# A first transfer of 4 rows ahead of the 16-row transfers in a DMA-fed relu-and-sum kernel

## The chip, the cores and the metric

The kernel runs on one core of one Trainium2 chip. In what follows, ACT is the scalar engine, DVE the vector engine, and SP the engine that here only issues transfers. A chunk is the rows that one transfer brings to a buffer. A transfer lands when its semaphore, a counter that engines wait for, tells that all its data are there.

The metric is device time in microseconds (us). Every run quoted here was fast (granted clock 1.0 in all), so only like runs are compared. The profile covers a span about 1.5 us shorter than the device time (161.4 us against 162.92 in the run profiled before). Times within a profile count from the start of that span.

## The reference

```python
x = np.random.randn(32, 512, 1024).astype(np.float32)   # 67.1 MB
relu_x = np.maximum(x, 0)
out = np.sum(relu_x, axis=-1).astype(np.float32)         # one number per row of 1024
```

There are 16384 rows, so 128 rows on each of the 128 partitions. A row is 4 KB. Each byte is read once and used once.

## The kernel before

The rows of a partition lie one behind the other in memory, so "16 rows per partition" is one run of 64 KB per partition. Seven transfers of 16 rows go round three buffers. A tail of 8, 4, 2 and 1 rows and two half rows follows in one of those buffers (the last half row in a small array of its own), so that little compute is left after the last byte.

```python
BIG = 16; NBIG = 7; NTWO = 6; NB = 3
STEPS = [4, 5, 7]; MIXED = [3, 4, 5]; TAIL = [8, 4, 2, 1]; LAST = [512, 512]

tb = NBIG % NB
for c in range(NBIG + 1):                       # issued from SP
    if c >= NB:
        sp.wait_ge(s_dve, 3 * (c - NB + 1))     # the chunk three earlier is consumed
    if c < NBIG:
        sp.dma_start(out=buf[:, c % NB, :, :],
                     in_=xv[:, c * BIG : (c + 1) * BIG, :]).then_inc(s_in[c], 16)
# ... tail transfers into buf[:, tb], each with a semaphore of its own ...

for c in range(NTWO):                           # chunks 0 to 5
    b, steps = c % NB, STEPS if c < NTWO - 1 else MIXED
    act.wait_ge(s_in[c], 16)
    # ... chunk 5: 2 rows go to DVE alone and 2 to ACT alone ...
    r = 0
    for i, n in enumerate(steps):
        t = buf[:, b, r : r + n, :]
        act.activation(t, t, AF.Relu).then_inc(s_act, 1)          # relu in place
        dve.wait_ge(s_act, 3 * c + i + 1)
        dve.tensor_reduce(out=res[:, c * BIG + r : c * BIG + r + n], in_=t,
                          axis=X, op=ALU.add).then_inc(s_dve, 1)  # sums of n rows
        r += n

for c in range(NTWO, NBIG):                     # chunk 6: row by row, both engines
    act.wait_ge(s_in[c], 16)
    dve.wait_ge(s_in[c], 16)
    for i in range(BIG):
        (on_act if i % 2 else on_dve)(*row(c, i))   # relu and sum in one instruction
# ... tail pieces the same way; the last half row is summed by DVE; then res goes out ...
```

## Time and profile before

The median was 162.84 us of 3 runs before the prediction, and 162.94 us of 4 with the run beside the result.

| What | Value | Read from |
|---|---|---|
| DMA engines busy | 97.0% of the span | page, queue part |
| DVE / ACT busy | 76% / 63% | page, busy part |
| 64 KB packet on one DMA engine | 2418 ns | the trace's packet records |
| First packet starts / last input packet ends | 1.73 / 158.5 us | the same |
| Last input to the end of the span | about 3 us | chain of waits, timeline |

From the page of the kernel before: busy time by engine, the busy tenths of the DMA engines and their rate in 40 equal slices of 4.03 us, and the queue's share of 16 engines' span.

```profile
DVE 122.0 (76%) x56; ACT 101.0 (63%) x55; POOL 0.2 (0%) x4
...
DMA  7969979979979979979979979979979979899992
GB/s 260 504 292 504 471 341 487 487 325 487 487 325 487 471 309 520 471 309 520 487 309 504 487 325 487 487 325 487 487 325 487 487 325 487 374 422 414 406 406 74
...
q1 hardware_dynamic: 2016, 67.18, 97.0%
```

A packet is booked in the slice in which it starts. A 64 KB packet lasts more than half a slice, so the rate swings between 300 and 500. The swings are no holes: the busy share is 97%.

SP waits by the waits view (engine and line, whom it waited for, us in total, times, longest). SP issues the transfers:

```profile
SPq L58 <- DVE res L101: 99.9, 4, 42.8
SPq L132 <- DVE last L82: 34.7, 1, 34.7
SPq L64 <- DVE res L101: 19.0, 1, 19.0
```

This looks like a transfer queue held up by DVE, and it is not. The list of DMA issues gives, for the seven 16-row transfers, the median time from issue to landing:

```profile
buf<-in_x_dram SPq DMA_DIRECT2D x7, 36.4
```

The movement of one such transfer takes about 19.4 us (8 packets of 2418 ns on each engine). It lands 36.4 us after its issue because about 17 us of earlier transfers are queued ahead of it.

The end of the chain of waits (start us, us, what), and four lines of DVE's timeline near the end (start us, us, the instruction, and in brackets the idle time before it and what ended that). The first line of the second fence is the first row of chunk 6, then come the first row of the 8-row piece, the first of the 4-row piece, and the last half row.

```profile
124.16 34.13 DMA buf<-in_x_dram
158.29 0.02 issue
158.31 0.73 ACT buf L79 x2
159.04 0.02 issue
159.07 0.69 DVE last L82 x2
```

```profile
139.27 1.22 DVE L82 TENSOR_SCALAR_CACHE_REDUCE buf<-buf 128x1024 f32<-128x1024 f32 x1 [1.74 <-DMA buf<-in_x_dram]
...
148.99 1.22 DVE L82 TENSOR_SCALAR_CACHE_REDUCE buf<-buf 128x1024 f32<-128x1024 f32 x1 [0.51 <-DMA buf<-in_x_dram]
...
153.88 1.22 DVE L82 TENSOR_SCALAR_CACHE_REDUCE buf<-buf 128x1024 f32<-128x1024 f32 x1 [0.25 <-DMA buf<-in_x_dram]
...
159.07 0.69 DVE L82 TENSOR_SCALAR_CACHE_REDUCE last<-last 128x513 f32<-128x513 f32 x1 [0.19 <-ACT buf L79]
```

DVE waits for data before every piece: it keeps up. The compute that nothing hides is the last half rows' (0.73 and 0.69 us). The start of the kernel, by contrast, shows the two engines idle for a long time: ACT's first activation starts at 23.13 us, DVE's first reduction at 26.78.

```profile
23.13 14.04 ACT L99 ACTIVATE buf<-buf 128x4096 f32<-128x4096 f32 x3 [21.13 <-DMA buf<-in_x_dram]
26.78 9.85 DVE L101 TENSOR_REDUCE res<-buf 128x4 f32<-128x4096 f32 x2 [26.78 <-ACT buf L99]
```

### The profile page before, as it was taken

How to read it: one execution, taken by the hardware profiler on the slowest of the kernel's cores; microseconds unless marked ns; L12 is line 12 of the kernel's file. 1: busy time of each engine (PE TensorE's matmuls, PEld its weight loads, DVE VectorE, ACT ScalarE, POOL GpSimd, SP SyncE). 2: the span in 40 equal slices, each digit the busy share in tenths (PEclk: the TensorE clock that was granted, in tenths of full speed). 3: DMA queues.
4: the chain of work that ended last, by engine and by line, in shares of the span. 5: the costliest groups of instructions: out<-in, count | busy, mean ns of one | idle time of the engine just before them, and what ended most of it. 6: DMA issues, size and time to landing. Idle time of an engine off the chain costs nothing.

```text
span 161.4 us, 143 instructions
## 1 busy us (share of the span) xinstructions
DVE 122.0 (76%) x56; ACT 101.0 (63%) x55; POOL 0.2 (0%) x4
## 2 busy tenths in 40 slices
DVE  0000003998969898798979989699899999598995
ACT  3000029992499906998089960999429980496972
POOL 0000000000000000000000000000000000000000
DMA  7969979979979979979979979979979979899992
GB/s 260 504 292 504 471 341 487 487 325 487 487 325 487 471 309 520 471 309 520 487 309 504 487 325 487 487 325 487 487 325 487 487 325 487 374 422 414 406 406 74
DMA packets 2016, 67.18 MB, mean 416 GB/s; under 512 B 224, under 2 KB 352, under 8 KB 736
## 3 DMA queue, kind: packets, MB, share of 16 engines
q1 hardware_dynamic: 2016, 67.18, 97.0%
HBM read 67.11 MB, written 0.07 MB: 416 GB/s over the span
## 4 chain that ended last, share of the span: by engine, by line
DMA 69%; ACT 18%; DVE 10%; SPq 1%; issue 0%
DMA buf<-in_x_dram 69%; ACT buf L99 17%; DVE res L101 9%; SPq L64 1%; ACT buf L79 0%; DVE last L82 0%; SPq L58 0%
## 5 line engine op out<-in xcount | busy, mean ns | idle before, releaser
L101 DVE TENSOR_REDUCE res<-buf 128x4 f32<-128x4096 f32 (+3 forms) x18 | 100.4, 5603 | 34.9 <-ACT buf L99 34.9
L99 ACT ACTIVATE buf<-buf 128x4096 f32<-128x4096 f32 (+3 forms) x18 | 80.8, 4553 | 47.7 <-DMA buf<-in_x_dram 47.7
L79 ACT ACTIVATE buf<-buf 128x1024 f32<-128x1024 f32 (+1 forms) x18 | 18.4, 1021 | 9.7 <-DMA buf<-in_x_dram 9.7
L82 DVE TENSOR_SCALAR_CACHE_REDUCE buf<-buf 128x1024 f32<-128x1024 f32 x18 | 21.0, 1217 | 2.7 <-DMA buf<-in_x_dram 2.5
L79 ACT ACTIVATION_READ_ACCUMULATOR buf<-buf 128x1 f32 x18 | 3.4, 187 | 0.0
L99 ACT ACT_TABLE_LOAD x1 | 1.3, 1283 | 0.7 <-PEq L147 0.7
L82 DVE DVE_READ_ACCUMULATOR buf<-buf 128x1 f32 x18 | 1.5, 84 | 0.0
L82 DVE TENSOR_SCALAR_CACHE_REDUCE last<-last 128x513 f32<-128x513 f32 x1 | 0.7, 690 | 0.2 <-ACT buf L79 0.2
L147 POOL MEMSET const-bfloat16-1.0<- 128x1 bf16 x1 | 0.1, 102 | 0.0
L147 POOL MEMSET const-uint8-127<- 128x1 uint8 x1 | 0.1, 101 | 0.0
L147 POOL MEMSET const-float32-0.0<- 128x1 f32 x1 | 0.1, 99 | 0.2 <-issue 0.2
L147 POOL MEMSET const-float32-1.0<- 128x1 f32 x1 | 0.1, 98 | 0.0
L82 DVE DVE_READ_ACCUMULATOR last<-last 128x1 f32 x1 | 0.1, 83 | 0.0
## 6 DMA issues: line engine op xcount, KB each, us to landing
buf<-in_x_dram SPq DMA_DIRECT2D x1, 4096.0 KB, 26.7
buf<-in_x_dram SPq DMA_DIRECT2D x1, 2048.0 KB, 31.2
buf<-in_x_dram SPq DMA_DIRECT2D x1, 1024.0 KB, 33.2
buf<-in_x_dram SPq DMA_DIRECT2D x1, 512.0 KB, 34.0
buf<-in_x_dram SPq DMA_DIRECT2D x1, 256.0 KB, 34.1
last<-in_x_dram SPq DMA_DIRECT2D x1, 256.0 KB, 34.3
buf<-in_x_dram SPq DMA_DIRECT2D x7, 36.4
out_dram<-res SPq DMA_DIRECT2D x1, 64.0 KB, 1.5
```

Of the source, the lines that this page charges most:

```text
L64: sp.dma_start(out=buf[:, tb, r : r + n, :], in_=xv[:, NBIG * BIG + r : NBIG * BIG + r + n, :],).then_inc(s_in[NBIG + i], 16)
L79: return act.activation(t, t, AF.Relu, accum_out=acc)
L82: return dve.tensor_scalar(out=t, in0=t, scalar1=0.0, scalar2=None, op0=ALU.max, op1=ALU.add, accum_out=acc)
L99: act.activation(t, t, AF.Relu).then_inc(s_act, 1)
L101: dve.tensor_reduce(out=res[:, c * BIG + r : c * BIG + r + n], in_=t, axis=X, op=ALU.add).then_inc(s_dve, 1)
L147: nc = _bacc.Bacc("TRN2", target_bir_lowering=False, num_devices=1)
```

## The change

The change goes after that idle start. A small transfer of 4 rows is sent first, into the third buffer, and both engines compute it while chunk 0 arrives. All later chunks begin 4 rows further on, and the seventh is 12 rows instead of 16. The third 16-row transfer must now wait until the four first rows have been used, since they lie in its buffer.

```diff
+FRONT = 4
+SHORT = BIG - FRONT
...
+    sp.dma_start(out=buf[:, NB - 1, 0:FRONT, :], in_=xv[:, 0:FRONT, :]).then_inc(s_front, 16)
     for c in range(NBIG + 1):
+        if c == NB - 1:
+            sp.wait_ge(s_fdone, 2)
         if c >= NB:
             sp.wait_ge(s_dve, 3 * (c - NB + 1))
         if c < NBIG:
+            n = BIG if c < NTWO else SHORT
             sp.dma_start(
-                out=buf[:, c % NB, :, :], in_=xv[:, c * BIG : (c + 1) * BIG, :]
+                out=buf[:, c % NB, 0:n, :],
+                in_=xv[:, FRONT + c * BIG : FRONT + c * BIG + n, :],
             ).then_inc(s_in[c], 16)
...
+    act.wait_ge(s_front, 16)
+    dve.wait_ge(s_front, 16)
+    for i in range(FRONT):
+        f = on_act if i % 2 else on_dve
+        ins = f(buf[:, NB - 1, i, :], res[:, i : i + 1])
+        if i >= FRONT - 2:
+            ins.then_inc(s_fdone, 1)
...
-        for i in range(BIG):
+        for i in range(SHORT):
             (on_act if i % 2 else on_dve)(*row(c, i))
```

Cut: the shifted columns of `res`, and index changes of the same kind in the tail.

More of the change, by code (lines that the diff above doesn't have):

```diff
@@ L47, in bass_relu_sum_kernel @@
     s_tdve = nc.alloc_semaphore("s_tdve")
+    s_front = nc.alloc_semaphore("s_front")
+    s_fdone = nc.alloc_semaphore("s_fdone")
     s_out = nc.alloc_semaphore("s_out")
@@ L57, in bass_relu_sum_kernel @@
         if c < NBIG:
+            n = BIG if c < NTWO else SHORT
             sp.dma_start(
-                out=buf[:, c % NB, :, :], in_=xv[:, c * BIG : (c + 1) * BIG, :]
+                out=buf[:, c % NB, 0:n, :],
+                in_=xv[:, FRONT + c * BIG : FRONT + c * BIG + n, :],
             ).then_inc(s_in[c], 16)
     r = 0
+    j0 = NBIG * BIG
     tail = []
@@ L65, in bass_relu_sum_kernel @@
             out=buf[:, tb, r : r + n, :],
-            in_=xv[:, NBIG * BIG + r : NBIG * BIG + r + n, :],
+            in_=xv[:, j0 + r : j0 + r + n, :],
         ).then_inc(s_in[NBIG + i], 16)
@@ L86, in row @@
     def row(c, i):
-        return buf[:, c % NB, i, :], res[:, c * BIG + i : c * BIG + i + 1]
+        return buf[:, c % NB, i, :], res[:, FRONT + c * BIG + i : FRONT + c * BIG + i + 1]
+    act.wait_ge(s_front, 16)
[5 more added lines that the diff above has]
+            ins.then_inc(s_fdone, 1)
     for c in range(NTWO):
@@ L101, in bass_relu_sum_kernel @@
             dve.tensor_reduce(
-                out=res[:, c * BIG + r : c * BIG + r + n], in_=t, axis=X, op=ALU.add
+                out=res[:, FRONT + c * BIG + r : FRONT + c * BIG + r + n], in_=t, axis=X, op=ALU.add
             ).then_inc(s_dve, 1)
@@ L107, in bass_relu_sum_kernel @@
                 on_act(*row(c, i))
-    j0 = NBIG * BIG
     for c in range(NTWO, NBIG):
@@ L124, in bass_relu_sum_kernel @@
     act.wait_ge(s_in[-2], 16)
-    on_act(buf[:, tb, BIG - 1, 0 : LAST[0]], last[:, LAST[1] : LAST[1] + 1]).then_inc(s_tact, 1)
+    on_act(buf[:, tb, sum(TAIL), 0 : LAST[0]], last[:, LAST[1] : LAST[1] + 1]).then_inc(s_tact, 1)
     dve.wait_ge(s_tact, 1)
```

## The prediction

> **What bounds the kernel now.** The input transfers. The page's DMA queue part gives 97.0% of 16 engines' span of 161.4 us; DVE is busy 76%, ACT 63%. In the trace's packet records a 64 KB packet (one partition of a 16-row transfer) takes 2418 ns on one engine: 433 GB/s over 16. That agrees with the Trainium skill, "DMA: Bandwidth & Descriptors", section "Where 436 GB/s comes from" (435.2 GB/s). The first packet starts at about 2.0 us, the last input lands just before 158.3; in between no engine runs dry. The rest is fixed: 2 us before, 3 us after (chain of waits: ACT 0.73, DVE 0.69 us; output transfer 1.5 us from issue to landing).
>
> The 99.9 us that SP waits for DVE (SP waits view) cost nothing: a 16-row transfer lands 36.4 us after issue, its own movement takes 19.4, so it sits about 17 us behind queued data. ACT's 21.1 us before the first landing and its 5 us gaps later are idle time of engines that keep up: DVE needs 17.5 us per chunk (4.42 + 5.49 + 7.62), a chunk takes 19.4.
>
> **What the change removes, adds, moves.**
> - Same bytes. Per engine, 8 packets of 64 KB become 8 of 16 KB (611 ns each, seen in the tail) and 8 of 48 KB (about 1815 ns, interpolated): 2426 against 2418 ns, +0.06 us, plus one 9 ns semaphore packet.
> - The first rows land at 8 to 9 us instead of 23; both engines do two rows each (DVE 1.22, ACT 1.04 + 0.19 us a row) by about 11 us. Off the path.
> - Chunks 0 to 5 land 4.8 us later, so buffers free and issues come 4.8 us later; each still finds queued data, because everything ahead moved too. The third chunk now waits for the four first rows (about 11 us) while 16 MB are queued until about 45 us: no starving.
> - The short seventh transfer lands where the long one did (about 139 us). DVE finishes chunk 5 at about 142.3 instead of 137.5, starts the seventh 3 us late, but has 6 rows there instead of 8: done at about 149.2, when the 8-row tail lands (149.0). It has caught up by the 4-row landing (153.9). The ending is unchanged.
> - The first 16 packets now take 0.4 to 0.85 us longer than later ones. With 16 KB packets first, this start-up loss may change by a few tenths either way: the main uncertainty.
>
> **On the critical path:** about +0.07 us of DMA work; the earlier compute gains nothing, because only the last half rows' compute is on the path.
>
> **Predicted:** 162.9 us, 8 times in 10 between 162.5 and 163.4. Faster by over 2%: 0.01; within 2%: 0.98; slower: 0.01.
>
> **What would show the steps right or wrong.** DMA share about 97%, mean about 416 GB/s. The timeline shows ACT and DVE starting at 8 to 9 us. SP still waits about 100 us for DVE, harmlessly. The chain of waits ends as before: DMA to about 158.3, ACT 0.73, DVE 0.69. DVE's idle before the seventh transfer's rows disappears; its idle before the 4-row, 2-row and last rows stays. GB/s by slice shows no new hole.
>
> **What would make it wrong.** An issue that comes too late (the third transfer behind the first rows' compute) and leaves a hole in the DMA row; DVE not catching up before the last pieces; a start-up that is cheaper or dearer with 16 KB packets; or 16 KB packets running slower at the start, where all engines begin together, than in the tail.

## The result, and the profile after

The changed kernel took 162.73 us in the median (162.4 to 162.9, 4 runs) against 162.94 (162.8 to 163.17). The ratio is 0.9983, with a 95% interval from 0.9962 to 1.0004. Ratios here are the mean time of one kernel's fast runs over that of the other's of the same rounds, so they are not quite the ratio of the medians. The engines start earlier, as the change meant them to, and the time stayed.

The page of the changed kernel:

```profile
DVE 121.9 (75%) x56; ACT 101.1 (63%) x55; POOL 0.2 (0%) x4
...
DMA  5979989989999999998999998998998999898991
GB/s 191 589 341 438 487 373 438 487 373 438 487 390 422 487 406 406 487 422 390 487 422 390 487 438 373 487 455 357 487 455 353 487 402 414 373 487 378 410 402 45
...
q1 hardware_dynamic: 2160, 67.18, 96.9%
```

The DMA share is unchanged, with 144 more packets (128 for the new transfer's partitions, 16 for its semaphore). No slice between the first and the last is empty.

The start, in its timeline: compute begins at 8.07 us, 15 us earlier. Then DVE waits again, 21.30 us, because chunk 0 now lands at 28.09 instead of 23.13.

```profile
8.07 1.06 ACT L90 ACTIVATE buf<-buf 128x1024 f32<-128x1024 f32 x1 [6.06 <-DMA buf<-in_x_dram]
8.07 1.22 DVE L93 TENSOR_SCALAR_CACHE_REDUCE buf<-buf 128x1024 f32<-128x1024 f32 x1 [8.07 <-DMA buf<-in_x_dram]
...
28.09 14.04 ACT L117 ACTIVATE buf<-buf 128x4096 f32<-128x4096 f32 x3 [17.84 <-DMA buf<-in_x_dram]
31.74 9.85 DVE L119 TENSOR_REDUCE res<-buf 128x4 f32<-128x4096 f32 x2 [21.30 <-ACT buf L117]
```

SP's waits: the third transfer's new wait (8.4 us, until about 10 us) is there, and the rest is a few us shorter than before (96.0 against 99.9, 29.8 against 34.7).

```profile
SPq L67 <- DVE res L119: 96.0, 4, 39.0
SPq L149 <- DVE last L93: 29.8, 1, 29.8
SPq L75 <- DVE res L119: 19.0, 1, 19.0
SPq L67 <- DVE buf L93: 8.4, 1, 8.4
```

The six 16-row transfers land as long after their issue as before:

```profile
buf<-in_x_dram SPq DMA_DIRECT2D x6, 36.3
```

The end of the chain of waits, and the same four DVE instructions as before:

```profile
129.09 29.27 DMA buf<-in_x_dram
158.36 0.02 issue
158.39 0.73 ACT buf L90 x2
159.12 0.02 issue
159.14 0.69 DVE last L93 x2
```

```profile
142.35 1.22 DVE L93 TENSOR_SCALAR_CACHE_REDUCE buf<-buf 128x1024 f32<-128x1024 f32 x1
...
149.18 1.23 DVE L93 TENSOR_SCALAR_CACHE_REDUCE buf<-buf 128x1024 f32<-128x1024 f32 x1
...
153.98 1.22 DVE L93 TENSOR_SCALAR_CACHE_REDUCE buf<-buf 128x1024 f32<-128x1024 f32 x1
...
159.14 0.69 DVE L93 TENSOR_SCALAR_CACHE_REDUCE last<-last 128x513 f32<-128x513 f32 x1 [0.17 <-ACT buf L90]
```

The last half row starts at 159.14 us, against 159.07 before. One thing did move: the brackets at the first three instructions are gone. DVE starts chunk 6 at 142.35 instead of 139.27, and it catches up with the data only at the 4-row piece. So the engines' early start came back as a later finish of the middle chunks: 4.8 us of transfer now stand before each of them.

### The profile page after: what moved, and what is told of

It is laid out like the page before. It is cut to its first block, busy times and chain, and to the rows that moved or that the text cites. A ratio compares the mean times of both kernels' runs of the same rounds, so it can differ in the third digit from the quotient of the medians.

```text
span 161.4 us, 144 instructions
## 1 busy us (share of the span) xinstructions
DVE 121.9 (75%) x56; ACT 101.1 (63%) x55; POOL 0.2 (0%) x4
## 3 DMA queue, kind: packets, MB, share of 16 engines
q1 hardware_dynamic: 2160, 67.18, 96.9%
## 4 chain that ended last, share of the span: by engine, by line
DMA 69%; ACT 18%; DVE 10%; SPq 2%; issue 0%
DMA buf<-in_x_dram 69%; ACT buf L117 17%; DVE res L119 9%; SPq L75 1%; ACT buf L90 0%; DVE last L93 0%; SPq L67 0%; SPq L59 0%
## 6 DMA issues: line engine op xcount, KB each, us to landing
buf<-in_x_dram SPq DMA_DIRECT2D x6, 36.3
```

## The experiments

The theory is that the input transfers set the time, and that compute and issue both have slack which the change moves about without exceeding it. One rival is that the early start has a real gain, partly cancelled by a cost of the change. The other, which the idle start suggests, is that such a head start pays whenever compute matters.

### Is the small ratio real? (e1_again, e12_again: the changed kernel, unedited)

> The changed kernel itself, in more rounds, to see whether the small ratio of 0.998 is real. Theory (the input transfers bound the kernel, everything else is hidden): ratio to the kernel before 0.998 to 1.001, no difference beyond 0.3 us; in both profiles the last input lands within 0.2 us of the same instant. Rival (the change has a real gain of the early start which a small loss partly cancels): a ratio clearly under 0.998 whose interval leaves out 1.

> The changed kernel once more, beside the repeat. Theory: ratio to the kernel before between 0.998 and 1.002. Rival (a real gain of 0.2 us or more): under 0.999 with an interval that leaves out 1.

The first gave 162.86 us in the median and a ratio of 1.0000 (0.9981 to 1.0020). One of its signs missed: the last input packet ended at 158.20 us against 158.48 before, 0.28 us apart where 0.2 was allowed. The second gave 162.50 and 0.9975 (0.9960 to 0.9991), which lies just outside the theory's range, leaves out 1 and is what the rival expected. The three sets of runs give 0.9983, 1.0000 and 0.9975. A gain of 0.1 to 0.2% is possible, and 2% is far outside. The same program moved by 0.45 us in the mean (162.94 and 162.50), which is as much as the effect in question. The kernel before did not move with it (means of 162.9 in both), so a gain of this size is not excluded either.

### Taking the early compute away (e2_late_compute, e11_late_again)

The transfers stay split, but both engines wait for chunk 0 before they compute the four first rows:

```diff
     act.wait_ge(s_front, 16)
     dve.wait_ge(s_front, 16)
+    act.wait_ge(s_in[0], 16)
+    dve.wait_ge(s_in[0], 16)
     for i in range(FRONT):
```

> Keeps the split transfers but takes the head start away: both engines wait for the first 16-row transfer too before they compute the four first rows (at about 28 us instead of 8). Theory: the early compute is worth nothing, so within 0.3 us of the changed kernel; the third transfer is issued at about 31 us instead of 10, still before the queued data end at about 46 us. Rival (an early-start gain of up to about 1 us is there and hides a loss): slower than the changed kernel by that gain.

> A repeat, because the first run of this kernel was 0.4 us slower in the median than the changed kernel, against the 0.3 us that the theory allowed. In that profile the 64 KB packets between 4 and 8 us were slower (0.42 us per engine in all, against 0.06 to 0.09), in a stretch where no compute runs in either kernel; the profile of the run with the early gate shows the same, though its program is the changed kernel's up to there. Theory (such packet times vary from execution to execution): the order of the two is not kept, difference within 0.3 us. Rival (early compute is worth some 0.3 to 0.4 us): again 0.3 us or more slower than the changed kernel of the same call.

The first run had a median of 163.25 us and a ratio to the kernel before of 1.0019 (1.0004 to 1.0035). The second had 162.84 us and 1.0007 (0.9986 to 1.0028). In the timeline of the first, the first rows are computed from 28.27 us, and the third 16-row transfer is issued at 31.72 (the last line shows two issues together).

```profile
28.27 1.22 DVE L93 TENSOR_SCALAR_CACHE_REDUCE buf<-buf 128x1024 f32<-128x1024 f32 x1 [28.27 <-DMA buf<-in_x_dram]
...
31.72 21.91 SPq L67 DMA_DIRECT2D buf<-in_x_dram  x2
```

So a 20 us later first compute costs at most a few tenths. But the theory's limit of 0.3 us was missed twice: this kernel was slower than the changed kernel by 0.39 us and by 0.34 us in the medians (0.31 and 0.45 us in the means). Most of it lies outside the profiled span. Each run's span is on record, to 0.1 us. Device time less span is 1.87 and 1.78 us in the mean for this kernel, against 1.58 and 1.55 for the changed kernel and 1.52 and 1.53 for the kernel before. So 0.29 of the 0.31 us and 0.23 of the 0.45 us are not in the stretch where the kernel's transfers and compute run. Within it the late compute cost 0.02 and 0.22 us. What is longer outside is not shown.

The profiles don't settle the rest. In the first one, the last input packet ended at 158.64 us and 64 KB packets between 4 and 8 us were slow by 0.44 us per engine in all. In the second it ended at 158.10 us, earlier than in any profile of the changed kernel (158.20 to 158.55), and that slow stretch was gone. This edit also issues the third transfer 21 us later, so the two are not told apart. Whether the early compute is worth up to 0.2 us within the span, and what adds the time outside it, stays open.

### How late may the third transfer be? (e3_gate_early, e4_gate_late)

The third 16-row transfer waits for more of chunk 0's DVE steps:

```diff
             sp.wait_ge(s_fdone, 2)
+            sp.wait_ge(s_dve, 2)        # e3_gate_early;  3 in e4_gate_late
```

> The third 16-row transfer also waits for the second of chunk 0's three DVE steps, so it is issued at about 41.6 us. The first 36 rows keep the DMA engines fed until about 46.2 us (2.0 + 36 x 1.21 + 0.5). Theory: 4 to 5 us to spare, so no difference from the changed kernel (within 0.3 us). Rival (SP waits are costs of themselves): slower by part of the 31 us of later issue.

> The third 16-row transfer waits for the last DVE step of chunk 0, so it is issued at about 49.8 us, 3.6 us after the queued data end. Theory: a hole of 3.6 + 1.2 (issue to first packet) = 4.8 us in the DMA row, plus about 0.5 us of slow first packets; nothing later can win it back, so about 168 us (167 to 168.7). Rival (compute and transfers have slack that absorbs a hole): under 165 us.

With the early gate SP waited 39.7 us for it, and the median was 163.19 us, ratio 1.0008 (0.9991 to 1.0024). That is 0.33 us above the changed kernel's median, just past the theory's 0.3, and 0.12 in the means. It is not clear of noise. With the late gate SP waited 48.0 us, only 8.3 us more, and the median was 168.72 us, ratio 1.0364 (1.0341 to 1.0386). The DMA rate of the late gate, and the DMA share and rate in two stretches of it (stretch, its length, DVE, ACT and POOL busy with instruction counts, clock, DMA share, GB/s):

```profile
GB/s 196 557 424 329 502 455 377 424 486 424 345 0 298 455 502 408 345 502 502 377 377 502 471 314 471 502 408 345 502 502 333 471 388 377 439 455 400 426 401 92
```

```profile
46.00:52.00 6.00, 4.70 (x2) 4.29 (x2) 0.00 (x0) 1.00 0.46 153
52.00:140.00 88.00, 76.42 (x18) 61.41 (x14) 0.00 (x0) 1.00 0.98 424
```

This is what a real hole looks like: a slice with 0 GB/s. From the packet records, all engines stand still from 47.4 to 51.1 us. The average engine idled 5.43 us between the first and the last input packet of all engines, against 0.68 in the changed kernel. The difference is the 4.8 us expected. Its packets took 0.9 us longer, 0.67 of which lies in slow packets between 48 and 56 us, at the restart. Together these are the 5.6 us by which the last input packet ended later (164.19 against 158.55). Nothing won them back. The cliff lies between the two gates, which issued the third transfer at 41.9 and 50.2 us. In the late gate's profile the engines ran out of queued packets between 45.8 and 47.4 us. The change's own wait, over by about 10 us, is far from it.

Doing away with that wait by a buffer for the first rows alone was tried too. It did not build: 16384 bytes per partition were needed and 16224 were left. With the queue full until about 46 us, little was to be expected of it.

### A kernel where compute is the limit (e5_before_dve2, e6_after_dve2, e7_split_dve2)

Every DVE reduction of chunks 0 to 5 is done twice, the first time into an array that nobody reads. The outputs stay correct. In the kernel before:

```diff
+            dve.tensor_reduce(
+                out=scrap[:, c * BIG + r : c * BIG + r + n], in_=t, axis=X, op=ALU.add
+            )
             dve.tensor_reduce(
                 out=res[:, c * BIG + r : c * BIG + r + n], in_=t, axis=X, op=ALU.add
             ).then_inc(s_dve, 1)
```

e7_split_dve2 is that doubled kernel before with another head start. Chunk 0 comes in two transfers, and its first step needs only the first of them:

```diff
-        if c < NBIG:
+        if c == 0:
+            sp.dma_start(out=buf[:, 0, 0:4, :], in_=xv[:, 0:4, :]).then_inc(s_half, 16)
+            sp.dma_start(out=buf[:, 0, 4:BIG, :], in_=xv[:, 4:BIG, :]).then_inc(s_in[0], 16)
+        elif c < NBIG:
...
-        act.wait_ge(s_in[c], 16)
+        act.wait_ge(s_half if c == 0 else s_in[c], 16)
...
+            if c == 0 and i == 1:
+                act.wait_ge(s_in[0], 16)
```

> The kernel before with every DVE reduction of the first six chunks done twice (the first copy goes to a scrap array): DVE now needs 35 us per chunk against 19.4 of transfer, so compute bounds it. From the durations: DVE starts at 26.8, 5 x 35.0 + 28.8 + 16 rows of 1.14 + 0.7 and the end: about 253 us (250 to 256), DVE busy without gaps from 26.8 us on. It is the yardstick for the next two.

> The changed kernel with the same doubling. Theory of the head start: the two rows that DVE does early are worth 2.3 us, but chunk 0 lands 4.8 us later and DVE is idle in between, so about 2.7 us SLOWER than the doubled kernel before even though compute bounds it (1.5 to 3.5 us). Rival (the head start is worth the earlier start of the engines, and shows as soon as compute is on the path): faster, by 2.3 us (the rows done early) up to 18.7 us (8.1 against 26.8 us start).

> The doubled kernel before with another head start: chunk 0 itself comes in two transfers, 4 and 12 rows, and its first step needs only the first; nothing else is later. Theory: DVE does the first step (8.8 us doubled) from about 11.7 us and the rest from about 27.6 instead of 35.6: about 8 us faster than the doubled kernel before (6 to 9), some 245 us.

The medians were 249.24 us, 252.13 us and 241.26 us. The first missed its range (250 to 256). Instructions that follow each other without a wait start closer together than their durations: 4.34 us for the listed 4.42, 7.53 for 7.61. The estimate added durations: over 36 reductions, 0.08 us each make 2.9 of the 3.8 us that it was too long. The two differences came as expected: +2.9 us for the change's head start and -8.0 us for the other.

DVE's timeline of the three, at the start, in this order:

```profile
26.54 4.42 DVE L102 TENSOR_REDUCE scrap<-buf 128x4 f32<-128x4096 f32 x1 [26.54 <-ACT buf L100]
30.88 4.41 DVE L105 TENSOR_REDUCE res<-buf 128x4 f32<-128x4096 f32 x1
35.21 5.48 DVE L102 TENSOR_REDUCE scrap<-buf 128x5 f32<-128x5120 f32 x1
```

```profile
9.44 1.22 DVE L94 TENSOR_SCALAR_CACHE_REDUCE buf<-buf 128x1024 f32<-128x1024 f32 x1
10.58 0.08 DVE L94 DVE_READ_ACCUMULATOR buf<-buf 128x1 f32 x1
31.80 4.42 DVE L120 TENSOR_REDUCE scrap<-buf 128x4 f32<-128x4096 f32 x1 [21.14 <-ACT buf L118]
```

```profile
11.99 4.42 DVE L108 TENSOR_REDUCE scrap<-buf 128x4 f32<-128x4096 f32 x1 [11.99 <-ACT buf L106]
16.32 4.41 DVE L111 TENSOR_REDUCE res<-buf 128x4 f32<-128x4096 f32 x1
27.33 5.49 DVE L108 TENSOR_REDUCE scrap<-buf 128x5 f32<-128x5120 f32 x1 [6.60 <-ACT buf L106]
```

From the first reduction on, DVE doesn't wait again in the first two kernels, so that start sets their time. The change moves two rows (2.28 us of DVE) to the front and puts off that start by 5.26 us (31.80 against 26.54): 2.98 us lost, where 2.9 were measured. It doesn't help even where compute is the limit, since all chunks behind it come later and DVE idles in between. The split delays nothing: 4 rows are done while the other 12 arrive, and the 5-row step starts at 27.33 instead of 35.21, 7.88 us earlier, where 8.0 were measured.

Here the doubled kernel moves only 271 GB/s over its span. The Trainium skill, "Perfetto Trace Analysis", section "DMA Optimizations", says of splitting transfers into smaller chunks that it may help if DMA engines are generally idle. This agrees: here the DMA engines are busy for 64.5% of the span and idle for long stretches, and the split brought 8.0 us. What the page does not say, these runs show: at 97% DMA share the same split brought nothing clear of noise (next experiment).

### The better-shaped head start on the real kernel (e8_split)

This is the same split of chunk 0 on the kernel before, with nothing doubled.

> The kernel before (nothing doubled) with chunk 0 in two transfers of 4 and 12 rows, the better-shaped head start. Theory: the transfers bound the kernel, so it is worth nothing: ratio to the kernel before 0.997 to 1.002. Rival: if any head start of compute pays, this one does, since it delays nothing: faster by 0.5 us or more.

The median was 162.77 us, ratio 0.9987 (0.9972 to 1.0003). Even a head start that costs nothing brings nothing clear of noise while the transfers are the limit. This and the changed kernel are the best of the kernels tried, and neither is clearly better than the kernel before.

### DVE's slack at the end (e9_before_pad, e10_after_pad)

One useless reduction of 4 rows is put on DVE just before chunk 6, in both kernels:

```diff
         act.wait_ge(s_in[c], 16)
+        dve.tensor_reduce(
+            out=scrap[:, 0:4], in_=buf[:, (NTWO - 1) % NB, 0:4, :], axis=X, op=ALU.add
+        )
         dve.wait_ge(s_in[c], 16)
```

> The kernel before with one more DVE reduction of 4 rows (4.42 us, into a scrap array) between the sixth and the seventh chunk, to measure DVE's slack at the end. In its trace DVE idles 1.7 us before the seventh chunk and about 1.1 us in pieces before the later ones. Theory: 2.7 to 2.9 us are absorbed and about 1.5 us show (164.0 to 164.9 us).

> The changed kernel with the same 4.42 us in the same place. In its trace DVE runs without a gap from chunk 5 to the 4-row tail piece and idles only about 0.6 us in all after that. Theory: about 3.8 us show (166 to 167 us), some 2.3 us more than in the padded kernel before: the change used up DVE's slack at the end without cost so far. Rival (the change left the end of the kernel as it was): both padded kernels the same within 0.3 us.

The medians were 164.13 us (ratio 1.0074) and 166.80 us (1.0245). The same added work costs about 1.2 us in the kernel before and about 4 us in the changed one (its medians elsewhere are 162.50 to 162.86). Some 0.2 us of both lie outside the span again (device time less span is 1.79 and 1.83 us), so the trace is the better measure. The last DVE instruction of the padded kernel before, then of the padded changed kernel:

```profile
160.11 0.68 DVE L83 TENSOR_SCALAR_CACHE_REDUCE last<-last 128x513 f32<-128x513 f32 x1
```

```profile
162.68 0.68 DVE L94 TENSOR_SCALAR_CACHE_REDUCE last<-last 128x513 f32<-128x513 f32 x1
```

Both start without a wait: now DVE ends the kernel. Against the unpadded 159.07 and 159.14, they are later by 1.04 and 3.54 us. The addition took 4.33 us from start to start, so 3.29 us were absorbed before the change and 0.79 after. The timelines say the same. DVE's rows follow each other every 1.14 us when nothing holds them, and what the starts of chunk 6 and the tail exceed that by, with the 1.74 us before chunk 6, adds up to 3.29 us before and 0.84 us after the change. The change used up three quarters of DVE's slack at the end, and the time didn't show it. The rival (the end as it was) falls.

The first of the two was expected to show 1.5 us and showed 1.04 in the trace, because the expectation added the bracketed idle times. Those leave out pauses under about 0.15 us and the 0.08 us in which DVE reads out the sum.

## Why the prediction was right

- **What bounds it: right.** DMA share 97.0 and 96.9%, last input packet ending at 158.48 and 158.55 us. (The first packet, put at about 2.0 us, began at 1.73 by the packet records.) Doubling DVE's work and delaying a transfer showed what it takes to change the limit.
- **Size of the cost: consistent, not resolved.** 16 KB and 48 KB packets took 611 and 1815 ns in the median as estimated, so +0.06 us. The last input packet did end 0.07 us later in these two profiles, but that agreement is luck: it ended anywhere from 158.20 to 158.55 us in three profiles of the changed kernel.
- **Compute starts at 8 to 9 us, off the path: right on the first part.** It started at 8.07. On the second part it is right within a few tenths: the late-compute runs were 0.02 and 0.22 us longer within the span, and the rest of their 0.31 and 0.45 us lies outside it, unexplained.
- **No starving at the third transfer: right.** It was issued after about 10 us, and the cliff lies past 41.9 us.
- **Later issues still find queued data: right.** The transfers land 36.3 us after issue, before 36.4, and no slice is empty.
- **DVE catches up by the 4-row piece: right, and close.** Predicted: start of chunk 6 at 142.3, done at 149.2. In the trace its last row of chunk 6 hands over at 149.18. The signs named for it were half right. The idle before chunk 6 did vanish, but "its idle before the 4-row, 2-row and last rows stays" isn't what the waits view lists: of DVE's three waits for data at the end (2.5 us) none is left there; the one that it lists is the 8.1 us at the start. Pauses of 0.25 us and less are left in the timeline.
- **Start-up: no change seen.** The first 16 packets took 0.07 to 0.85 us longer than 2418 ns before, and 0.29 to 0.81 us longer than 611 ns after. (The prediction gave 0.4 to 0.85 for before; two of the sixteen lay below, at 0.07 and 0.39.) The last engine began at 2.97 us before and 2.44 after. The end shows nothing of it.

What the prediction did not spell out: the change eats slack. It saw DVE start chunk 6 3 us late and catch up, and called the ending "unchanged". That is true of the time, but not of the 3.29 us of DVE slack, of which 0.8 are left.

## What to carry to other kernels

Long idle time at the start of an engine is worth something only if that engine ends the kernel. Look first at whether the transfers, from first packet to last, leave a hole. Judge a head start by when the first full chunk can start, not by when the first instruction does: four rows sent ahead delayed every later chunk and lost 2.9 us where compute was the limit, while splitting the first chunk in place won 8.0. An unchanged time doesn't mean unchanged slack, so measure the slack with an added instruction before you build the next change on it.

## What the Trainium skill lacked or had wrong

- "DMA: Bandwidth & Descriptors", "Where 436 GB/s comes from": agrees. From 32 to 64 KB a packet takes 1205 ns longer (2418 against 1213), which is 27.2 GB/s per engine and 435 over 16, leaving 8 ns fixed per packet. The same page's specifications put the HBM limit per core at about 358 GB/s. One core alone got 416 over the whole span, as the page's note on single-core numbers allows.
- The same page, "Latency and other measured facts", gives about 600 ns as the first-byte time for transfers issued from SP. Here the first packet began 1.00 us after the first issue started (0.73 to 1.73 us) and 0.63 us after it ended, so the figure holds if it is counted from the end; the last of the 16 engines began at 2.44 to 2.97 us. The page has no figure for that spread, nor for the first packet of each engine being up to 0.85 us longer.
- The same section's row on row pitches at large powers of two gives 207 GB/s for a pitch of 512 KiB, for copies within HBM. It doesn't say whether loads to SBUF suffer. Here the partitions lie 512 KiB apart, and packets of 16 to 64 KB ran at 26.8 to 27.1 GB/s per engine.
